# A bidirectional mLSTM and neighbourhood-attention layer on one core: masks by POOL's selection, convolutions that pause at two places, token-major tiles evicted in pairs

## The chip, the cores and the metric

The kernel runs on one core of one Trainium2 chip. The metric is the device time of one execution in microseconds (us). The kernel before was timed three times: median 2721.96 us, lowest 2721.62, highest 2723.16. Durations below come from one profiled execution of it, whose own time was 2718.74 us, with a span from first to last instruction of 2717.0 us.

Engines are named as in the profile: PE is TensorE's matrix multiplication and PEld its weight load; DVE is VectorE, ACT is ScalarE, POOL is GpSimd, SP is SyncE, which issues most DMAs.

## What is computed

One encoder layer runs over two sequences, a prompt of 1024 tokens (s=0 in the code) and a sample of 2048 (s=1), each with 16 learned meta tokens in front. One input projection feeds two branches; their gated outputs are projected, merged and projected again. Cut to its core:

```python
xn = _rmsnorm(h, g_pre)
proj = xn @ w_in + b_in
na_q, na_k, na_v, na_z, ml_qk, ml_v, ml_z, ml_o, ml_g, mg = split(proj)
ya = (neighbourhood_attention(na_q, na_k, na_v, na_rpb) * silu(na_z)) @ w_a
yb = (mlstm_branch(ml_qk, ml_v, ml_g, ml_o, conv_w, head_g) * silu(ml_z)) @ w_b
ga, gb = split(sigmoid(mg), 2)
out = h + _rmsnorm((ga * ya + gb * yb) @ w_out, g_post)
```

In the mLSTM branch, q and k first go through a convolution of three taps and a silu. Then, for each of 4 heads and each of two directions, in chunks along the sequence:

```python
logD = where(lower, b[:, None] - b[None, :] + ig[None, :], NEG)
S = (q @ k.T) * exp(logD - m_t[:, None])
num = S @ v + e_inter * (C @ q)
den = sum(S) + e_inter * (n @ q)
h = num / maximum(abs(den), exp(-m_t))
```

The two directions are added, gated by a sigmoid, and normalised per head (mean and variance over 128 features). `where(lower, ...)` is what the text calls the mask. In the kernel it is applied to the exponent: entries outside the triangle become about -1e30, so that their exponential is 0.

## The kernel before

**Numbers.** Values are float32, and a product of two of them is made as three matmuls of parts: each operand is split into a high part (a copy in the type `fp32r`, made by ACT) and a low part (the difference, made by DVE). In the trace a split shows as a pair such as `whi`/`wlo`, `xh`/`xl`, `sh`/`sl`, `vh`/`vl`.

**Two streams on PE.** A dense stream (`PLAN`) does the projections: first the group of s=0 with a few column blocks, then a stream of seven-product units (`sstream`, L1036 on, where a 2 by 2 block product is made of seven products instead of eight) for the other columns of s=0, then groups of s=1 in two halves of 1024 tokens, and at the end the output projections. A sparse stream (`STEPS`) does the mLSTM of s=0, the attention of s=0, the mLSTM of s=1 and the attention of s=1. `run` takes pieces of both in turn, by costs written in the code, and what comes out is PE's order.

**What sets the order.** PE's instructions stay in the order in which the code is run. The order on the other engines is made by a list scheduler, which simulates the program with durations of its own; an instruction given to `self.behind` stays in program order among its engine's. So an edit that leaves PE alone can still rearrange DVE, ACT, POOL and SP.

**Beside the dense stream.** After each piece of dense work the code calls `beside` (L530). It advances up to two convolutions of q and k (`cprep`, L1546, by `pstep`, L1588): a load, a scaled copy on ACT (L1567), two multiply-adds on DVE (L1570), a tanh on ACT (L1572), a product on DVE (L1574), and stores. It makes one step per call, and a second once a result of the first group of s=1 exists.

**Token-major tiles** (`tm_unit`, L619). For columns that are stored with tokens on partitions, a tile of 128 tokens by 256 or 264 columns is summed in a PSUM bank of 512 words (tag `pj`, three banks). For s=1 DVE adds the bias and moves the tile to SBUF (`stT<-pj,bb`, L661), one tile at a time, two into each `stT` buffer. Of the columns of the attention's values, POOL then issues eight DMAs per buffer (`nv<-stT`, L1034).

**Splitting x at a group change** (`build_half`, L512 to 518): four steps, each with a copy on ACT and a subtraction on DVE (`xh`, `xl`).

**mLSTM outputs** (`ml_outputs`, L1721). A head's sequence is cut into blocks of 256 tokens (two chunks of 128). For each block and both directions at once, 128 partitions by 2 chunks by 2 directions by 128:

- `load`: q and k, the values, and by DMA a broadcast of the decay exponents into `um`.
- `mask` (L1758): DVE adds `trim`, the two triangles of 0 and -1e30, to `um`, pinned by `self.behind`. `trim` is loaded once per sequence from the input `trimask`.
- `decay` (L1764): four exponentials on ACT, in place in `um`.
- `scores` (PE, L1799 and L1801), read out as `ss` (L1803, L1804).
- `weigh`: the product `um<-um,ss` (DVE, L1813), split into `sh` (ACT, L1814) and `sl` (DVE, L1815).
- `back` (PE): `tr` from the state, `sm` from `sh`, `sl` and the values; then `num` (ACT L1829, DVE L1834).
- `finish`: the denominators (L1841 to L1844) and `hb` (L1851, L1852). After every second block `ml_norm` (L1895 on) normalises 512 tokens: `hb<-tog,hb`, four BATCH_NORM_STATS2 and four BATCH_NORM_AGGREGATE, a reciprocal root by twelve tiny operations, `nb` (L1912), four `hb` on ACT (L1914), and a last product with `szg` on DVE (L1915).

The blocks overlap: while block b-1 is in `back`, block b is in `scores` and `weigh`, and block b+1 in `mask` and `decay`.

Of the kernel before, what the change touches and what calls it, by code (L numbers as in the profile page):

```python
# [10 lines left out]
F32 = mybir.dt.float32  # L11
# [3 lines left out]
ALU = mybir.AluOpType  # L15
# [3 lines left out]
P = 128  # L19
TCARGS = dict(schedule_with_timeline_sim=True)  # L20
D = 1024
KT = D // P
# [6 lines left out]
BIG = 1e30  # L29
# [97 lines left out]
class K:  # L127
# [3 lines left out]
    def __init__(self, tc, ins, outs):  # L131
        self.tc, self.nc = tc, tc.nc
        self.xs = []
        self.i, self.o = ins, outs
        self.wreq, self.wraw, self.wrdy, self.wout = deque(), deque(), deque(), 0
        self.wseen, self.wkept, self.xkept = set(), {}, {}
        self.rwait = {}
        self.xput, self.turn, self.last, self.turns = deque(), 0, None, False
        self.need, self.gpost = False, None
        self.pq, self.pact = deque(), deque()  # L140
        self.have, self.rtag = {}, "tr"
        self.fmend = {C_MK + 3 * P: "a", C_NK + 3 * P: "k", C_NQ + 3 * P: "q", C_NZ + 3 * P: "z"}
        self.bg, self.XF, self.XS, self.sb, self.staged = deque(), {}, {}, {}, deque()
        self.hold, self.early = deque(), True
        self.rpre, self.xhold = {}, True


    def rsqrt8(self, pool, v, shape):
# [292 lines left out]
    def build_half(self, s, t0, res):  # L441
# [26 lines left out]
        if s == 0:  # L468
            xts = self.xnext or [self.xtload(s, t0, e, wp, 4) for e in range(4)]
            self.xnext = None  # L470
            while self.rwait:
                yield "wait"
            self.early = False
            yield "scaled"
            g = self.gpre
            if not self.done:
                p = self.psum("sm", [P, 512])
                nc.tensor.matmul(p[:, :KT], self.ident, g, start=True, stop=True)
                g = self.cp.tile([P, KT], F32, name="gx")
                nc.vector.tensor_copy(g, p[:, :KT])  # L480
            x, r = self.xparts(), []
            for e in range(4):
                self.xsplit(x, xts[e], e, 0, g)
                if not self.done:
                    self.wflush(2)
                yield
            res.append(tuple(x))
            if self.done:
                return
            yield from self.rsum(self.toks, r)  # L490
            nc.vector.tensor_copy(self.rc[:, 4:8], r[0])
            dg = self.rdiag(r[0], self.toks[0][0])

            def rows():
                self.rrows(dg, self.rr[:, 1], "sm")
                self.xp.close()
            self.rwait[s, t0] = rows
        else:
            xts = [self.xtload(s, t0, e, wp, 4) for e in range(4)]
            yield  # L500
            yield
            rr = wp.tile([P, 512], F32, name="rx", tag="thT", bufs=1)
            self.rrows(self.rpre.pop((s, t0)), rr, self.rtag)
            yield
            for k in range(KT):
                v = xts[k // 2][:, k % 2]
                self.behind(nc.vector.scalar_tensor_tensor(v, v, self.gpre[:, k:k + 1], rr, op0=ALU.mult, op1=ALU.mult))
                if k % 2:
                    yield
            yield "scaled"  # L510
            x = self.xparts(t0 % 1024 == 0)
            for e in range(4):  # L512
                h = x[0][:, 2 * e:2 * e + 2, :512]
                self.behind(nc.scalar.activation(h, xts[e], AF.Copy))
                self.behind(nc.vector.tensor_tensor(x[1][:, 2 * e:2 * e + 2, :512], xts[e], h.bitcast(F32), op=ALU.subtract))
                yield
            res.append(tuple(x))
            self.xkeep(s, t0, x)

# [10 lines left out]
    def beside(self):  # L530

        self.turn += 1
        self.pstep()
        if (1, 0) in self.have:
            self.pstep()
        if self.bg and self.turn % 2 == 0:
            if next(self.bg[0], "end") == "end":
                self.bg.popleft()
        if self.xput and self.turn % 2 and not self.xhold:
            self.behind(self.nc.sync.dma_start(*self.xput.popleft()))  # L540
# [78 lines left out]
    def tm_unit(self, col, halves, wd):  # L619
# [9 lines left out]
                todo.append((x, s, 0, NM, 1, None))  # L629
        for j, (x, s, c, n, cnt, tok) in enumerate(todo):  # L630
            st = wp.tile([P, 2, WU], F32, name="stT", bufs=4)
            for a in range(cnt):
                p = self.psum("pj", [P, 512])
                o = p[:n, :wd]
                xs = slice(c + a * P, c + a * P + n)
                for k in range(KT):
                    wh, wl = ws[k // 4][0][:, k % 4, :], ws[k // 4][1][:, k % 4, :]
                    if tok is None:
                        both = [(p[:48, :wd], self.xmm[:, k, :], wh), (o, self.xmm[:, k, :NM], wl)]
                        for y, (out, lhs, rhs) in enumerate(both if k < KT - 1 else both[::-1]):  # L640
                            nc.tensor.matmul(out, lhs, rhs, start=k == y == 0, stop=k == KT - 1 and y == 1, skip_group_check=True)
                    else:
                        xh, xl = x[0][:, k, xs], x[1][:, k, xs]
                        nc.tensor.matmul(o, xh, wh, start=k == 0, stop=False)  # L644
                        nc.tensor.matmul(o, xh, wl, start=False, stop=False)  # L645
                        nc.tensor.matmul(o, xl, wh, start=False, stop=k == KT - 1)  # L646
                    if k == 3:
                        if j == len(todo) - 1 and a == cnt - 1:
                            self.wdone()
# [7 lines left out]
                elif s == 0:  # L657
                    r = tok // P + a
                    nc.vector.scalar_tensor_tensor(st[:n, a, :wd], p[:n, :wd], self.rc[:n, r:r + 1], bb[:n, :wd], op0=ALU.mult, op1=ALU.add)
                else:  # L660
                    nc.vector.tensor_tensor(st[:n, a, :wd], p[:n, :wd], bb[:n, :wd], op=ALU.add)  # L661
                if a == cnt - 1:
                    self.tm_store(col, wd, s, n, cnt, tok, st)
                yield 12 * C256
# [371 lines left out]
    def sstream(self, visits, nxt):  # L1036
# [9 lines left out]
        for n, u in self.sorder(visits):  # L1046
# [15 lines left out]
                            self.sstage(*visits[v + 1][:2], w)  # L1062
            q = self.sq[n]
            if u == 7 and not n:
                self.sbload(1)
            tm = c in TMAJ
            form = ("p (k c) -> p k c", dict(k=4)) if tm else ("p (a k c) -> p a k c", dict(a=2, k=4))
# [95 lines left out]
    def group(self, s, t0, meta, cols, reuse, nxt):  # L1163
# [4 lines left out]
        for j, (kind, c) in enumerate(jobs):  # L1168
# [21 lines left out]
            for hf in range(2):  # L1190
# [2 lines left out]
                    side = self.spread(self.build_half(*todo[1][:2], self.xs), 15)  # L1193
                elif last and nxt and nxt[0] == "S":
                    if hf == 0:
                        while self.bg:
                            if next(self.bg[0], "end") == "end":
                                self.bg.popleft()
# [398 lines left out]
    def ml(self, s):  # L1597
# [3 lines left out]
        with tc.tile_pool(name=f"mg{s}", bufs=1, side="right", reuse_waits="tile") as keep:  # L1601
            with tc.tile_pool(name=f"mt{s}", bufs=1, side="right", reuse_waits="tile") as mp:
                self.tri = keep.tile([P, 2, P], F32, name="tri")
                nc.sync.dma_start(self.tri, self.i["tri"])
                self.trim = keep.tile([P, CB, 2, P], F32, name="trim")
                for j in range(CB):
                    nc.sync.dma_start(self.trim[:, j], self.i["trimask"])
                g = []
                yield from self.ml_gates(s, keep, mp, g)
            with tc.tile_pool(name=f"ml{s}", bufs=1, side="right", reuse_waits="tile") as mp:  # L1610
# [110 lines left out]
    def ml_outputs(self, mp, s, h, g, NB, sts, norms):  # L1721
# [33 lines left out]

        def mask(b):
            if b < NB:
                self.behind(nc.vector.tensor_tensor(ums[b], ums[b], self.trim, op=ALU.add))  # L1758

        def decay(b):  # L1760
            if b < NB:
# [505 lines left out]
```

## Time and profile before

| | |
|---|---|
| median of 3 runs | 2721.96 us (2721.62 to 2723.16) |
| profiled execution | 2718.74 us |
| its span | 2717.0 us, 47583 instructions |
| mean granted clock of PE | 0.998 of full speed |
| DMA | 657.53 MB, mean 242 GB/s |

The page's next lines give the chain of work that ended last, followed back from the last instruction, in shares of the span:

```profile
PE 88%; DMA 7%; DVE 2%; ACT 2%; issue 1%; SPq 1%; POOL 0%; DVEq 0%; ACTq 0%; POOLq 0%
```

A row of a timeline begins with the start and the duration in us; then come engine, source line, operation and tiles (out<-in). Brackets give the time for which the engine had been idle ahead of it, and what ended that. Rows of groups give the count, the busy time with the mean ns of one, and the idle time with its releasers.

### The profile page before, as it was taken

How to read it: one execution, taken by the hardware profiler on the slowest of the kernel's cores; microseconds unless marked ns; L12 is line 12 of the kernel's file. 1: busy time of each engine (PE TensorE's matmuls, PEld its weight loads, DVE VectorE, ACT ScalarE, POOL GpSimd, SP SyncE). 2: the span in 40 equal slices, each digit the busy share in tenths (PEclk: the TensorE clock that was granted, in tenths of full speed). 3: DMA queues.
4: the chain of work that ended last, by engine and by line, in shares of the span. 5: the costliest groups of instructions: out<-in, count | busy, mean ns of one | idle time of the engine just before them, and what ended most of it. 6: DMA issues, size and time to landing. Idle time of an engine off the chain costs nothing.

```text
span 2717.0 us, 47583 instructions
## 1 busy us (share of the span) xinstructions
PE 2686.7 (99%) x16696; PEld 2394.5 (88%) x16696; DVE 1766.1 (65%) x4376; ACT 1520.2 (56%) x3375; POOL 126.0 (5%) x294
## 2 busy tenths in 40 slices
PE   9999999999999999999999999999999999999998
PEld 7999988879998889998878888888879898989988
DVE  5557765535777747775424857574658879687864
ACT  5233354435555656666535757564648686767641
POOL 0005000005000013000000000000000000000000
PEclk9999999999999999999999999999999999999999
DMA  9984454369865797757486666786599999898955
GB/s 369 340 283 143 138 187 158 102 239 343 265 222 174 264 325 227 229 175 234 144 294 191 222 202 209 262 278 201 163 299 332 313 298 295 245 317 244 324 208 220
DMA packets 351507, 657.53 MB, mean 242 GB/s; under 512 B 53444, under 2 KB 158868, under 8 KB 351268
## 3 DMA queue, kind: packets, MB, share of 16 engines
q1 hardware_dynamic: 344004, 645.46, 71.7%
q0 software_dynamic: 7264, 9.04, 1.2%
q8 instruction: 131, 2.15, 0.3%
q14 instruction: 108, 0.88, 0.1%
HBM read 438.64 MB, written 215.66 MB: 241 GB/s over the span
## 4 chain that ended last, share of the span: by engine, by line
PE 88%; DMA 7%; DVE 2%; ACT 2%; issue 1%; SPq 1%; POOL 0%; DVEq 0%; ACTq 0%; POOLq 0%
PE pj L172 14%; PE pj L173 14%; PE pj L174 14%; PE pj L644 5%; PE pj L645 5%; PE pj L646 5%; PE sm L1407 3%; PE pj L2042 2%; PE pj L2044 2%; PE pj L2043 2%; PE tr L1393 2%; PE sm L174 2%; PE sm L173 2%; PE sm L172 2%; DMA wraw<-wu 1%; DMA wlo<-wl 1%
## 5 line engine op out<-in xcount | busy, mean ns | idle before, releaser
L172 PE MATMUL pj<-xh,whi 128*128 128x512 f32 (+1 forms) x1480 | 580.2, 392 | 4.6 <-ACT st L569 3.6
L173 PE MATMUL pj<-xl,whi 128*128 128x512 f32 (+1 forms) x1480 | 565.8, 382 | 0.2 <-DVE xl L345 0.2
L174 PE MATMUL pj<-xh,wlo 128*128 128x512 f32 (+1 forms) x1480 | 565.1, 382 | 0.3 <-DVE wlo L272 0.3
L644 PE MATMUL pj<-whi,xh 128*128 128x256 f32 (+1 forms) x1152 | 330.9, 287 | 0.0
L174 PEld LDWEIGHTS pj<-xh,wlo 128*128 128x128 f32 x1480 | 278.2, 188 | 58.2 <-DVE wlo L272 0.6
L172 PEld LDWEIGHTS pj<-xh,whi 128*128 128x128 f32 x1480 | 278.5, 188 | 54.1 <-ACT st L569 4.4
L645 PE MATMUL pj<-wlo,xh 128*128 128x256 f32 (+1 forms) x1152 | 325.0, 282 | 0.6 <-DMA wlo<-wl 0.6
L646 PE MATMUL pj<-whi,xl 128*128 128x256 f32 (+1 forms) x1152 | 324.8, 282 | 0.0
L173 PEld LDWEIGHTS pj<-xl,whi 128*128 128x128 f32 x1480 | 278.8, 188 | 46.2 <-issue 0.7
L2042 PE MATMUL pj<-whi,mh 128*128 128x256 f32 x768 | 220.3, 287 | 0.0
L645 PEld LDWEIGHTS pj<-wlo,xh 128*128 128x128 f32 x1152 | 217.1, 188 | 0.9 <-DMA wlo<-wl 0.8
L644 PEld LDWEIGHTS pj<-whi,xh 128*128 128x128 f32 x1152 | 217.3, 189 | 0.4
L646 PEld LDWEIGHTS pj<-whi,xl 128*128 128x128 f32 x1152 | 217.0, 188 | 0.0
L2043 PE MATMUL pj<-wlo,mh 128*128 128x256 f32 x768 | 217.0, 283 | 0.0
L2044 PE MATMUL pj<-whi,mlo 128*128 128x256 f32 x768 | 216.9, 282 | 0.0
L1396 DVE TENSOR_TENSOR pts<-tr,pts 96x384 fp32r<-96x384 f32 (+2 forms) x192 | 118.5, 617 | 64.7 <-ACT pts L1395 63.8
L172 PE MATMUL pj<-yh,whi 128*128 128x512 f32 x384 | 154.2, 401 | 1.8 <-DVE tg L2009 1.1
L173 PE MATMUL pj<-yl,whi 128*128 128x512 f32 x384 | 151.0, 393 | 0.2 <-DVE yl L1420 0.2
L174 PE MATMUL pj<-yh,wlo 128*128 128x512 f32 x384 | 151.0, 393 | 0.0
L2043 PEld LDWEIGHTS pj<-wlo,mh 128*128 128x128 f32 x768 | 146.1, 190 | 1.0
L2042 PEld LDWEIGHTS pj<-whi,mh 128*128 128x128 f32 x768 | 146.0, 190 | 1.0
L2044 PEld LDWEIGHTS pj<-whi,mlo 128*128 128x128 f32 x768 | 145.9, 190 | 0.0
(459 smaller groups left out, 6171.7 us busy)
## 6 DMA issues: line engine op xcount, KB each, us to landing
whi<-wh SPq DMA_DIRECT2D x140, 512.0 KB
wlo<-wl SPq DMA_DIRECT2D x140, 512.0 KB
wraw<-wu SPq DMA_DIRECT2D x64, 512.0 KB
wh<-whi SPq DMA_DIRECT2D x64, 512.0 KB
wl<-wlo SPq DMA_DIRECT2D x64, 512.0 KB
gt<-st SPq DMA_DIRECT2D x96, 256.0 KB
tg<-gt SPq DMA_DIRECT2D x96, 256.0 KB
xt<-xt SPq DMA_DIRECT2D x32, 512.0 KB
```

Source lines behind the costliest of these rows:

```text
L172: mm(out, ah, bh, start=start, stop=False, **more)
L173: mm(out, ah, bl, start=False, stop=False, **more)
L174: mm(out, al, bh, start=False, stop=stop, **more)
L644: nc.tensor.matmul(o, xh, wh, start=k == 0, stop=False)
L645: nc.tensor.matmul(o, xh, wl, start=False, stop=False)
L646: nc.tensor.matmul(o, xl, wh, start=False, stop=k == KT - 1)
L1393: nc.tensor.transpose(pt[:ks, ch, :], pr_[:, ch * ks:(ch + 1) * ks], self.ident)
L1396: nc.vector.tensor_tensor(pts[:ks, :nb, 1, :], pt[:ks, :nb], pts[:ks, :nb, 0, :].bitcast(F32), op=ALU.subtract)
L1407: nc.tensor.matmul(av[:, cb % 2], vt[:ks, kc // 8 + ch].rearrange("p a b -> p (a b)"), pts[:ks, ch].rearrange("p a b -> p (a b)"), start=c ...
L2042: nc.tensor.matmul(o, mh[:, f, xs], q, start=fresh and f == 0, stop=False, skip_group_check=True)
L2043: nc.tensor.matmul(o, mh[:, f, xs], w[1][:, k, :], start=False, stop=False, skip_group_check=True)
L2044: nc.tensor.matmul(o, ml[:, f, xs], q, start=False, stop=f == KT - 1, skip_group_check=True)
```

## The change

Three edits, and what the scheduler makes of them:

1. **Masks.** The addition of `trim` on DVE, 48 times 128x512, is replaced by `affine_select` on POOL, one for each direction of a block: 96 of 128x2x128. Each compares an affine function of partition and column with 0 and writes -1e30 where it is negative. They aren't pinned. The `trim` tile and its four loads go. POOL gets one more instruction ahead of the first select, which loads a library (the row `ISA`).
2. **Pauses.** A flag `quiet` stops the convolution steps of `beside` at two places: from the first half of the last unit of the group ahead of the seven-product stream until that stream's unit 7 of its first column block, and in the four steps that split x at a group change of s=1. In return, there is a third step per call once the mLSTM of s=0 is done.
3. **Pairs.** For s=1 and columns up to 256 wide, two token tiles share one PSUM bank, and DVE evicts both with one instruction of 128x2x256: 48 in place of 96 of 128x256.

PE keeps its instructions and their order. Three places of the other engines' lists:

**First place: POOL, the start of the first mLSTM** (names: `nv` is the store of the attention's values, `st` a state tile, `um` the exponents). Before:

```order
L1613 MEMSET va_6112 128x2
L1614 MEMSET va_6112 128x2
L1706 MEMSET st 128x130
L1034 DMA nv_244<-stT 8x8x128 x40
L1706 MEMSET st 128x130
L1034 DMA nv_244<-stT 8x8x128 x24
```

And now:

```order
L1711 MEMSET st 128x130
L1040 DMA nv_244<-stT 8x8x128 x24
L1765 ISA
L1765 AFFINE_SELECT um<-um 128x2x128 x2
L1040 DMA nv_244<-stT 8x8x128 x8
L1765 AFFINE_SELECT um<-um 128x2x128 x2
L1040 DMA nv_244<-stT 8x8x128 x32
L1765 AFFINE_SELECT um<-um 128x2x128 x4
```

The selects of the first blocks stand among the 64 DMA issues: 24 ahead of the first mask, 32 ahead of the second, all 64 ahead of the third and fourth.

**Second place: DVE, the start of the seven-product stream** (`cp` is a convolution, `sn` the first product's eviction, `wlo` the low part of a combined weight, `xl` that of a combined x). Before:

```order
L261 TENSOR_TENSOR wlo<-b_1815,whi 128x1024
L837 TENSOR_TENSOR b_1815<-b_1817,b_1815 128x1024
L557 TENSOR_TENSOR pj<-pj,rr 128x512
L1570 SCALAR_TENSOR_TENSOR cp<-cp,cw 128x272
L837 TENSOR_TENSOR t_2242<-b_1839,b_1815 128x1024
L1570 SCALAR_TENSOR_TENSOR cp<-cp,cw 128x272 x2
L959 TENSOR_TENSOR sn<-pj,bb 128x512
L1570 SCALAR_TENSOR_TENSOR cp<-cp,cw 128x272
L261 TENSOR_TENSOR wlo<-t_2242,whi 128x1024
```

And now:

```order
L843 TENSOR_TENSOR b_1815<-b_1817,b_1815 128x1024
L558 TENSOR_TENSOR pj<-pj,rr 128x512
L843 TENSOR_TENSOR t_2212<-b_1839,b_1815 128x1024
L261 TENSOR_TENSOR wlo<-t_2212,whi 128x1024
L558 TENSOR_TENSOR pj<-pj,rr 128x512
L261 TENSOR_TENSOR wlo<-b_1815,whi 128x1024
L558 TENSOR_TENSOR pj<-pj,rr 128x512
L261 TENSOR_TENSOR wlo<-b_2216,whi 128x1024
L778 TENSOR_TENSOR xl<-xt,xh 128x2x512
L965 TENSOR_TENSOR sn<-pj,bb 128x512
```

The four convolution operations are gone from there, and `wlo<-t` follows its `t` at once, ahead of `sn`.

**Third place: DVE and ACT, blocks 1 to 3 of the first head of the first mLSTM.** DVE before, from the eviction of a dense tile on (`ss` and `sc` are scores, `hb` the output of blocks 0 and 1; the row `um<-um,ss` is the product of block 2):

```order
L1844 RECIPROCAL den<-den 128x4
L1804 TENSOR_TENSOR ss<-ss,sc 128x256
L661 TENSOR_TENSOR stT<-pj,bb 128x264
L1852 SCALAR_TENSOR_TENSOR hb<-num,den,hb 128x128
L1813 TENSOR_TENSOR um<-um,ss 128x512
L1852 SCALAR_TENSOR_TENSOR hb<-num,den,hb 128x128
L1815 TENSOR_TENSOR sl<-um,sh 128x512
```

Now, from the next dense tile's eviction on, ahead of the product of block 2:

```order
L664 TENSOR_TENSOR stT<-pj,bb 128x264
L1859 SCALAR_TENSOR_TENSOR hb<-num,den,hb 128x128
L1906 SCALAR_TENSOR_TENSOR hb<-tog,hb 128x512
L1910 BN_STATS bs<-hb 128x6 x4
L1912 BN_AGGR mv<-bs 128x2 x4
L1914 TENSOR_SCALAR mv<-mv 128x4
```

then the tiny operations of the reciprocal root, of which the last and what follows are:

```order
L158 SCALAR_TENSOR_TENSOR nwy<-nwt,nwy 128x4
L1919 SCALAR_TENSOR_TENSOR nb<-mv,nwy 128x4
L1922 TENSOR_TENSOR hb<-hb,szg 128x512
L1820 TENSOR_TENSOR um<-um,ss 128x512
L1822 TENSOR_TENSOR sl<-um,sh 128x512
```

The whole normalisation, 23 instructions from `hb<-tog,hb` to `hb<-hb,szg`, has come ahead of the product of block 2. On ACT the exponentials of block 3 and `sh` of block 2 stood thus before:

```order
L1764 ACTIVATE um<-um,g_a_5902 128x128 x2
L1764 ACTIVATE um<-um,g_a_5908 128x128 x2
L1803 ACTIVATE ss<-sc 128x256
L1851 ACTIVATE hb<-num,den 128x128 x2
L432 ACTIVATE xsq,ss<-xr 128x1024
L689 ACTIVATE stT<-stT 128x528
L1814 ACTIVATE sh<-um 128x512
```

And now the exponentials of blocks 2 and 3, with `sh` of block 2:

```order
L1836 ACTIVATE num<-tr,g_eT_6066 128x130
L1921 ACTIVATE hb<-hb,nb,nwy 128x128 x4
L1771 ACTIVATE um<-um,g_a_5899 128x128 x2
L1771 ACTIVATE um<-um,g_a_5905 128x128 x2
L1771 ACTIVATE um<-um,g_a_5899 128x128 x2
L1771 ACTIVATE um<-um,g_a_5905 128x128 x2
L1821 ACTIVATE sh<-um 128x512
```

They stand behind the four `hb` of the normalisation. The order of all engines from the last third of the second mLSTM to the end is as before.

The diff:

```diff
@@ K.__init__
-        self.rpre, self.xhold = {}, True
+        self.rpre, self.xhold, self.quiet = {}, True, False
@@ build_half (s=1)
             x = self.xparts(t0 % 1024 == 0)
+            self.quiet = True
             for e in range(4):
...
                 yield
+            self.quiet = False
@@ beside
-        self.pstep()
-        if (1, 0) in self.have:
+        for _ in range(0 if self.quiet else 1 + ((1, 0) in self.have) + (("ml", 0) in self.done)):
             self.pstep()
@@ tm_unit
+            pair = s and tok is not None and 2 * wd <= 512
             for a in range(cnt):
-                p = self.psum("pj", [P, 512])
-                o = p[:n, :wd]
+                if not pair or not a:
+                    p = self.psum("pj", [P, 512])
+                o = p[:n, wd * a:wd * a + wd] if pair else p[:n, :wd]
...
-                        nc.tensor.matmul(o, xh, wh, start=k == 0, stop=False)
+                        nc.tensor.matmul(o, xh, wh, start=k == 0 and not (pair and a), stop=False, skip_group_check=True)
...
-                else:
+                elif not pair:
                     nc.vector.tensor_tensor(st[:n, a, :wd], p[:n, :wd], bb[:n, :wd], op=ALU.add)
+                elif a:
+                    two = bb[:, :wd].rearrange("p (t c) -> p t c", t=1).to_broadcast([P, 2, wd])
+                    nc.vector.tensor_tensor(st[:, :, :wd], p[:, :2 * wd].rearrange("p (t c) -> p t c", t=2), two, op=ALU.add)
@@ sstream
             if u == 7 and not n:
+                self.quiet = False
                 self.sbload(1)
@@ group (last unit ahead of "S")
                     if hf == 0:
+                        self.quiet = True
@@ ml
-                self.trim = keep.tile([P, CB, 2, P], F32, name="trim")
-                for j in range(CB):
-                    nc.sync.dma_start(self.trim[:, j], self.i["trimask"])
@@ ml_outputs
         def mask(b):
             if b < NB:
-                self.behind(nc.vector.tensor_tensor(ums[b], ums[b], self.trim, op=ALU.add))
+                for d in range(2):
+                    u = ums[b][:, :, d]
+                    nc.gpsimd.affine_select(u, u, [[0, CB], [1 - 2 * d, P]], ALU.is_ge, -BIG, base=0, channel_multiplier=2 * d - 1)
```

More of the change, by code (lines that the diff above doesn't have):

```diff
@@ L643, in tm_unit @@
                         xh, xl = x[0][:, k, xs], x[1][:, k, xs]
[L644 to L646 removed]
+                        nc.tensor.matmul(o, xh, wh, start=k == 0 and not (pair and a), stop=False, skip_group_check=True)
+                        nc.tensor.matmul(o, xh, wl, start=False, stop=False, skip_group_check=True)
+                        nc.tensor.matmul(o, xl, wh, start=False, stop=k == KT - 1, skip_group_check=True)
                     if k == 3:
```

## The prediction

> **What bounds the kernel now.** The page's busy shares come first, then the busy time by stage, cut where the kernel's own stages change: dense start to 212 us, seven-product stream to 565, first mLSTM (s=0) to 950, first attention to 1365, second mLSTM to 1975, second attention and output projection to the end. Columns: stretch, its length, then busy us of PE, PEld, DVE, ACT and POOL, the granted clock and the DMA share.
>
> ```profile
> PE 2686.7 (99%) x16696; PEld 2394.5 (88%) x16696; DVE 1766.1 (65%) x4376; ACT 1520.2 (56%) x3375; POOL 126.0 (5%) x294
> ...
> 0.00:212.00 212.00, 203.78 (x1348) 184.40 (x1349) 114.38 (x214) 85.93 (x143) 6.39 (x28) 1.00 0.90 325
> 212.00:565.00 353.00, 353.00 (x2016) 307.21 (x2015) 232.35 (x328) 158.13 (x234) 36.92 (x84) 1.00 0.48 155
> 565.00:950.00 385.00, 383.92 (x2664) 353.21 (x2663) 249.96 (x770) 205.34 (x515) 39.40 (x80) 1.00 0.73 248
> 950.00:1365.00 415.00, 414.44 (x2800) 382.23 (x2799) 248.28 (x584) 248.94 (x509) 37.53 (x74) 1.00 0.68 220
> 1365.00:1975.00 610.00, 608.06 (x3138) 509.44 (x3137) 366.98 (x1185) 352.59 (x920) 2.32 (x18) 1.00 0.69 226
> 1975.00:2717.00 742.00, 723.53 (x4741) 658.02 (x4739) 554.15 (x1299) 469.26 (x1055) 3.42 (x10) 0.99 0.87 283
> ```
>
> TensorE is the bound, at full clock. Its whole idle time is 2717.0 - 2686.7 = 30.3 us: 8.2 in the first stretch, 18.5 in the last, 1.1 and 1.9 in the two mLSTM stretches, 0.6 in the first attention, none in the stream. The change leaves TensorE's instructions and their order as they were. So it can win only a part of 30.3 us, and it loses wherever something that TensorE waits for comes later. Work taken from VectorE (65% busy) is no gain in itself.
>
> **Convolutions that pause (start of the seven-product stream).** The one place where the removed work stands ahead of TensorE:
>
> ```profile
> 207.99 0.50 DVE L1570 SCALAR_TENSOR_TENSOR cp<-cp,cw 128x272 f32<-128x272 f32 x1 [0.17 <-ACT cp L1567]
> 208.41 0.68 DVE L959 TENSOR_TENSOR sn<-pj,bb 128x512 f32<-128x512 f32 x1
> 209.01 0.49 DVE L1570 SCALAR_TENSOR_TENSOR cp<-cp,cw 128x272 f32<-128x272 f32 x1
> 209.24 0.36 PE L1079 MATMUL pj<-whi,xh 128*128 128x256 f32 x1 [0.89 <-DVE sn L959]
> 209.42 1.22 DVE L261 TENSOR_TENSOR wlo<-t,whi 128x1024 fp32r<-128x1024 f32 x1
> 210.69 0.38 PE L1080 MATMUL pj<-wlo,xh 128*128 128x256 f32 x1 [1.09 <-DVE wlo L261]
> ```
>
> TensorE sits 0.89 us for a weight part and a freed bank, and 1.09 us for `wlo`. Ahead of both, ACT and VectorE do convolution steps (0.50 and 0.49 us on VectorE, 0.17 waited for ACT). With the pause the splits `wlo` stand ahead of `sn` (second place of the change). I take both waits as gone: **-2.0** us. Bounds: 0 if the weight load itself is late, -2.0 at most, since there is nothing more to win here. The later catch-up (a third step once the first mLSTM is done) falls where TensorE idles 1.9 us in 610, on engines 58 to 60% busy (352.59 and 366.98 of 610.00): 0. The pause while x is split at the group change, four units of work long, I put at 0, bounds -0.6 and +1, by the 0.6 us idle in the stretch 950 to 1365.
>
> **Masks on POOL.** What leaves VectorE, and who waited for it:
>
> ```profile
> L1758 DVE TENSOR_TENSOR um<-um,trim 128x512 f32<-128x512 f32 x48 | 32.8, 683 | 5.1 <-DMA um<-ud 5.1
> ACT um L1764 <- DVE um L1758: 22.0, 22, 3.6
> 647.93 0.69 DVE L1758 TENSOR_TENSOR um<-um,trim 128x512 f32<-128x512 f32 x1 [1.51 <-DMA um<-ud]
> 656.61 0.68 DVE L1813 TENSOR_TENSOR um<-um,ss 128x512 f32<-128x512 f32 x1
> ```
>
> 48 adds of 0.683 us, 32.8 us of VectorE, go; 96 selects of 128x256 come. No row shows a select, so its price is bounded by POOL's nearest rows:
>
> ```profile
> L1706 POOL MEMSET st<- 128x130 f32 x8 | 1.7, 208 | 532.5 <-DVE ccl L1792 521.8 <-PE sm L173 10.7
> L1178 POOL CAST xmm<-xh 128x128 fp32r<-128x128 f32 x2 | 0.6, 350 | 3.2 <-ACT xh L391 3.2
> 171.00 1.28 POOL L587 COPY km<-st 128x16 f32<-128x16 f32 x1
> 171.01 1.22 DVE L772 TENSOR_TENSOR r0l<-xt,r0h 128x1024 fp32r<-128x1024 f32 x1
> ```
>
> The memset writes 130 elements a partition in 0.208 us and reads nothing: low end 0.2. The cast reads and writes 128 in 0.350; twice that is 0.7, the value I take, as the row with the most alike work. The copy of 16 elements took 1.28 us, exactly while VectorE ran a 1.22 us operation with two SBUF inputs: POOL can be held up for about that long. High end 0.35 + 1.28 = 1.6. Two selects a block then take 1.4 us (0.4 to 3.2) where the add took 0.68, so a mask comes some 0.7 us later. Cover: between the first mask at 647.93 and the product that needs its exponentials (656.61) lie 8.7 us; mask 0.7, exponentials 1.3 (ACT row below) leave 6.7. A library load for POOL, new ahead of the first select, has no row either; it stands behind 24 of the DMA issues and before `um` has landed at 647.9, in idle time. I put all of this at **+1.0** for TensorE, a small share of the 48 blocks being tight (bounds: 0, and the slow case among the rivals).
>
> The Trainium skill speaks against this move: its page "GPSIMD Engine Reference", section 1 (Specifications), says that POOL's SBUF interfaces are shared with VectorE and contended when a VectorE instruction has two SBUF inputs. The 1.28 us copy agrees. The same page, section 2.1 (Instruction dispatch), gives about 6 us for the first call of a freshly loaded kernel; no run here shows that, and by it, as an estimate, the sum stays the same, because the load lies in idle time of POOL.
>
> **Pairs.** 96 evictions of 128x256 at 0.42 us become 48 of 128x512 at the 0.68 of the `sn` row:
>
> ```profile
> L661 DVE TENSOR_TENSOR stT<-pj,bb 128x256 f32<-128x256 f32 x96 | 40.3, 420 | 27.9 <-PE pj L646 26.2 <-DMA nv<-stT 0.6
> ```
>
> 40.3 - 32.6 = 7.7 us of VectorE saved. VectorE waited for TensorE ahead of these (26.2 us), not the other way, so TensorE gains **0**; one bank held for two tiles costs nothing as long as the eviction follows within the next tile. Bounds -1.1 (all idle of that stretch) and +1.
>
> **What the new order costs.** With less work on VectorE the scheduler sets the first head of the first mLSTM out differently (third place of the change, VectorE and ACT): the product `um<-um,ss` of block 2 now stands behind the whole normalisation of query block 0, and ACT's exponentials of blocks 2 and 3 behind the four normalising `hb`. TensorE uses `sh` of block 2 in the first matmul of this list:
>
> ```profile
> 683.59 0.23 PE L172 MATMUL sm<-vh,sh 128*128 128x130 f32 x1
> ...
> 681.50 0.43 DVE L661 TENSOR_TENSOR stT<-pj,bb 128x264 f32<-128x264 f32 x1
> 681.92 0.35 DVE L1852 SCALAR_TENSOR_TENSOR hb<-num,den,hb 128x128 f32<-128x128 f32 x1
> 682.66 0.68 DVE L1899 SCALAR_TENSOR_TENSOR hb<-tog,hb 128x512 f32<-128x512 f32 x1
> 684.26 0.86 DVE L1903 BATCH_NORM_STATS2 bs<-hb 128x6 f32<-128x128 f32 x4
> 685.37 0.30 DVE L1905 BATCH_NORM_AGGREGATE mv<-bs 128x2 f32<-128x6 f32 x3
> 686.17 0.17 DVE L1905 BATCH_NORM_AGGREGATE mv<-bs 128x2 f32<-128x6 f32 x1
> 686.97 0.17 DVE L154 TENSOR_SCALAR nwy<-nwy 128x4 int32<-128x4 int32 x1
> 687.17 0.16 DVE L156 SCALAR_TENSOR_TENSOR nwt<-nwy 128x4 f32<-128x4 f32 x1
> 685.59 0.65 DVE L1815 TENSOR_TENSOR sl<-um,sh 128x512 fp32r<-128x512 f32 x1
> ...
> 692.59 1.64 ACT L1914 ACTIVATE hb<-hb,nb,nwy 128x128 f32<-128x128 f32 x4
> 671.39 1.28 ACT L1764 ACTIVATE um<-um,g_a 128x128 f32<-128x128 f32 x4 [1.33 <-DVE um L1758]
> 675.00 0.62 ACT L1814 ACTIVATE sh<-um 128x512 fp32r<-128x512 f32 x1
> ```
>
> In the run before, `sh` of block 2 was made at 675.00, 8 us early. In the new order the eviction of the dense tile at 681.50 stands ahead of the chain, and it can't come sooner, as TensorE fills that tile just then. From it on VectorE: eviction 0.43, `hb` 0.35, `hb<-tog,hb` 0.68, statistics 0.86, aggregates 0.30 + 0.17, then 13 tiny dependent operations 0.20 apart (686.97 to 687.17), 2.6: 5.4 us. On ACT: four `hb` 1.64, exponentials of blocks 2 and 3 at 1.28 each (the product of block 2 runs beside the second), `sh` 0.62: 4.8. A row begins some 0.08 us before the recorded end of the one ahead (`sn` above ends at 209.09, the next row begins at 209.01); eight such hand-overs take off 0.6. `sh` is there at 681.5 + 5.4 + 4.8 - 0.6 = 691.1. TensorE arrives at 683.59: a wait of 7.5. And `sl` (0.65, from `sh`) holds the third matmul of the group another 0.5, the first two filling the rest: **+8.0**, bounds 7 and 9.5 by the hand-overs. It doesn't hang on POOL: the last stores of NV are evicted and issued long before,
>
> ```profile
> 667.68 2.23 POOL L1034 DMA_DIRECT2D nv<-stT  x4 [0.23 <-DVE stT L661]
> ```
>
> so that with the eight issues of this eviction (at 0.56 each to 672.2) four selects even at 1.28 end at 677.3, when the exponentials can't start before 688.
>
> A long wait also costs clock behind it, as the one long wait of the last stretch shows:
>
> ```profile
> 2335.70:2339.30 3.60, 0.26 (x3) 0.02 (x1) 1.99 (x6) 3.54 (x9) 0.00 (x0) 1.00 1.01 195
> 2339.30:2342.70 3.40, 3.15 (x14) 3.16 (x15) 2.87 (x7) 3.40 (x12) 0.00 (x0) 0.50 1.04 222
> 2332.72 1.06 ACT L1344 ACTIVATE kd<-kr 64x1024 fp32r<-64x1024 f32 x1 [3.47 <-DMA kr<-nkm]
> ```
>
> After 3.3 us of idle TensorE ran 3.4 us at clock 0.50: 1.7 us lost. The new wait is longer, so **+1.7** once.
>
> **Sum.** -2.0 + 1.0 + 0 + 8.0 + 1.7 = +8.7 us on the profiled execution: 2718.74 + 8.7 = 2727.4. That execution lies 3.2 us below the median of the three runs; on the median, 2721.96 + 8.7 = **2730.7**, 0.32% slower. A measurement of this kernel can tell about 0.2% (5.4 us) from no change: slower is above 2727.4, faster below 2716.5.
>
> **The rivals.**
> *The tail gives it back (not slower).* The 3.3 us wait at 2335.7 and its 1.7 of half clock come from a `kr` load that landed late under a DMA share above 1. If the loads of the tail, shifted by the wait, fall apart again, 5.0 to 5.3 us go: 8.7 - 5.3 = +3.4, 2725.4. Against it: loads and TensorE shift together, and the order in the tail is the same on all engines. It decides if that load lands 3.3 us sooner against TensorE. 0.17.
> *The wait is half as long (not slower):* if ACT's and VectorE's chain starts earlier than I read, 4.0 and no half clock behind it, - 2.0 + 1.0 = +3.0, 2725.0. The eviction ahead of it stands against this. 0.04.
> *POOL is slow.* Selects held up by VectorE at 1.6 each put a mask 2.5 us later (3.2 for 0.68). The 6.7 us of cover hide that at the first block, but ACT waited for a mask 22 times, up to 3.6 us, so in these blocks it stood right behind. If a quarter of them, six, pass 2 us on to TensorE, it is +12 over the sum, 2742.7; if all 22 do, +44. The rule cited above is this rival's mechanism. It decides at a select above about 1.2 us, where a mask is 1.7 late. 0.12.
> *Faster (the change does what a relieved VectorE suggests, and the new order's wait doesn't appear, and the tail's goes):* -2.0 - 5.3 = -7.3, 2714.7. Only 30.3 us of idle exist at all, and both must happen. 0.05.
>
> **How the numbers follow.** Forecast 0.62, between 2728 and 2734 by the terms' own bounds. Slower: 0.62 + 0.12 = 0.74; within 0.2%: 0.17 + 0.04 = 0.21; faster 0.05. The range holds the forecast, both milder rivals (with 3 us for the start that doesn't gain or gains and for the spread of runs, 1.5) and the middle of the slow one: 2722 to 2743.
>
> **What would show it.** In the profile after: no wait of TensorE at `pj<-whi,xh` and `pj<-wlo,xh` near 209; one wait of 7 to 9 us near 683 (less the 2 us won before) at `sm<-vh,sh`, released by ACT's `sh`, with a stretch at half clock behind; selects at 0.4 to 1.0 us; idle of the later mLSTM stretch still near 2 us; the tail's wait for `kr` still there. I am wrong if `sh` of block 2 is ready before 684, if selects take over 1.2 us, or if TensorE waits for masks.

## The result and the profile after

| | before | with the change |
|---|---|---|
| median (runs) | 2721.62 us (5) | 2740.42 us (5) |
| lowest to highest | 2716.11 to 2723.16 | 2734.56 to 2746.08 |
| profiled execution, its span | 2718.74, 2717.0 us | 2740.42, 2738.5 us |

The ratio is 1.0076, 95% interval 1.0055 to 1.0097: slower by 18.8 us, where 9 were forecast. (Two single runs of nearly twice the time, 4979.61 us in e10 and 5337.15 us in the kernel before beside e5 to e8, are outside all ratios.) The page's busy shares of the changed kernel, then the three stretches that changed (columns as in the prediction):

```profile
PE 2695.3 (98%) x16696; PEld 2401.0 (88%) x16696; DVE 1743.9 (64%) x4280; ACT 1516.5 (55%) x3375; POOL 167.4 (6%) x390
```

and its windows:

```profile
565.00:950.00 385.00, 375.17 (x2608) 346.21 (x2607) 231.56 (x694) 198.29 (x501) 54.86 (x111) 0.99 0.70 239
950.00:1365.00 415.00, 409.47 (x2758) 378.27 (x2758) 253.45 (x585) 248.10 (x514) 37.41 (x74) 0.99 0.70 223
1365.00:1975.00 610.00, 605.46 (x3106) 505.52 (x3105) 341.05 (x1108) 342.35 (x896) 28.75 (x80) 1.00 0.67 221
```

TensorE's idle time went from 30.3 to 2738.5 - 2695.3 = 43.2 us, and its busy time, for the same matmuls, from 2686.7 to 2695.3. So the 21.5 us of span are 12.9 of waits and 8.6 in which the same matmuls kept TensorE busy longer. Of these 8.6, half clock behind the two longest waits makes 6.3, as shown below; the rest is in small pieces, such as matmuls that follow each other more slowly behind a short wait. Idle are 9.8 of 385 in the first mLSTM (1.1 before), 5.5 of 415 in the first attention (0.6) and 4.5 of 610 in the second mLSTM (1.9).

To see where it was lost, the same matmul is looked up in both timelines. TensorE's order is the same, so the difference of the starts is the delay up to there. Before:

```profile
785.59 0.39 PE L174 MATMUL sm<-vwh,kt 128*128 128x260 f32 x1 [0.34 <-DVE kt L1691]
1395.45 0.44 PE L1483 MATMUL sm<-g_lf,ones 128*1 128x68 f32 x4 [0.25 <-ACT g_aR L1476]
1717.82 0.39 PE L172 MATMUL sm<-vwh,kt 128*128 128x260 f32 x1 [0.33 <-ACT kt L1690]
2628.37 0.49 PE L172 MATMUL pj<-yh,whi 128*128 128x512 f32 x1 [0.67 <-ACT yh L1419]
```

With the change:

```profile
794.05 0.39 PE L174 MATMUL sm<-vwh,kt 128*128 128x260 f32 x1 [0.60 <-DVE kt L1696]
1412.85 0.44 PE L1491 MATMUL sm<-g_lf,ones 128*1 128x68 f32 x4 [0.25 <-ACT g_aR L1484]
1739.52 0.39 PE L172 MATMUL sm<-vwh,kt 128*128 128x260 f32 x1 [0.33 <-ACT kt L1695]
2650.18 0.49 PE L172 MATMUL pj<-yh,whi 128*128 128x512 f32 x1 [0.67 <-ACT yh L1427]
```

The delay is 8.5 us in the first mLSTM's second half, 17.4 at the start of the second mLSTM, 21.7 in its middle, 21.8 near the end. There are three losses, then, and the tail adds nothing. (The first is net of 2.9 us won ahead of it.)

**First loss, 8.5 us: the forecast one.** TensorE, ACT and POOL of the changed kernel around it:

```profile
688.38 0.48 PE L172 MATMUL sm<-vh,sh 128*128 128x130 f32 x1 [7.53 <-ACT sh L1821]
...
683.83 1.65 ACT L1921 ACTIVATE hb<-hb,nb,nwy 128x128 f32<-128x128 f32 x4 [2.31 <-DVE nb L1919]
685.38 2.43 ACT L1771 ACTIVATE um<-um,g_a 128x128 f32<-128x128 f32 x8
687.72 0.61 ACT L1821 ACTIVATE sh<-um 128x512 fp32r<-128x512 f32 x1
...
670.68 1.47 POOL L1765 TENSOR_SCALAR_AFFINE_SELECT um<-um 128x256 f32<-128x256 f32 x4
```

And its windows right behind the wait:

```profile
688.00:692.00 4.00, 3.58 (x15) 3.40 (x16) 3.13 (x11) 2.27 (x5) 0.00 (x0) 0.50 0.68 239
692.00:696.00 4.00, 4.00 (x23) 4.00 (x23) 2.04 (x10) 0.74 (x3) 0.00 (x0) 0.58 0.19 66
```

POOL had masked blocks 2 and 3 by 672.2. Their eight exponentials ran 13 us later, behind the four `hb` of the normalisation, and `sh` came 7.5 us late. Behind the wait the granted clock was 0.50 for 4 us and 0.58 on the mean of the next 4: 3.58 us of matmuls at 0.50 and 4 us at 0.58 lose about 3.5 us, not 1.7.

**Second loss, 8.9 us: the first attention.** No wait at all was forecast here. The chain of the changed kernel up to its second wait (start, duration, what):

```profile
1039.78 9.90 DMA cpl<-mq
1049.69 0.02 issue
1049.71 0.62 ACT cpl L1575
1050.34 0.03 issue
1050.36 0.63 DVE cpl L1578
...
1053.83 0.43 DVE yg L1422
```

Both waits in TensorE's timeline:

```profile
1026.87 0.74 PE L1415 MATMUL sm<-pts,vt 96*128 96x256 f32 x4 [1.18 <-ACT prb L1384]
1054.39 1.19 PE L1415 MATMUL sm<-pts,vt 96*128 96x256 f32 x4 [4.35 <-DVE yg L1422]
```

And the windows behind the second wait:

```profile
1054.40:1058.00 3.60, 3.60 (x17) 3.60 (x18) 2.71 (x6) 3.07 (x8) 1.28 (x3) 0.50 0.49 151
1058.00:1060.00 2.00, 2.00 (x10) 2.00 (x10) 1.16 (x3) 1.29 (x2) 2.00 (x4) 0.50 0.70 190
1060.00:1062.00 2.00, 2.00 (x17) 2.00 (x16) 1.69 (x5) 1.71 (x5) 1.15 (x3) 0.86 0.80 228
```

A convolution's load was in flight for 9.9 us. The convolution's first operation stood on ACT ahead of what the attention needed; VectorE took its multiply-adds and then the `yg` for which TensorE waited. With three steps a call the steps come closer together, and the distance between load and first use, counted in steps, is shorter in time: between 950 and 1365 us the median from a load's issue to the copy on ACT that reads it is 7.0 us with the change (7.0 in e1 too) and 15.8 before (16.5 in e2), when loads and copies are paired in order. Half clock again: 5.6 us at 0.50, 2.8 lost, and a little more in the third window.

**Third loss, 4.3 us: the second mLSTM.** SP's issue (SPq), POOL, ACT and TensorE of the changed kernel:

```profile
1607.99 0.73 SPq L1741 DMA_DIRECT2D um<-ud  x1
1615.04 0.77 POOL L1765 TENSOR_SCALAR_AFFINE_SELECT um<-um 128x256 f32<-128x256 f32 x2 [77.03 <-DMA wraw<-wu]
1615.48 1.28 ACT L1771 ACTIVATE um<-um,g_a 128x128 f32<-128x128 f32 x4 [3.64 <-POOL um L1765]
1616.66 0.36 ACT L1695 ACTIVATE kt<-tr 128x256 fp32r<-128x256 f32 x1
...
1617.07 0.39 PE L172 MATMUL sm<-vwh,kt 128*128 128x260 f32 x1 [1.74 <-ACT kt L1695]
```

The exponents land at about 1614.8, and ACT waits for them with `kt` behind it, on which TensorE depends: 1.74 us here, and 0.54 in the same way at 1473.63. In the kernel before, the addition was pinned on VectorE, and the exponentials of a new head stood behind the last `kt` on ACT. The selects aren't pinned, so the scheduler put the exponentials of two blocks further forward, ahead of the last two `kt`. Over the whole kernel ACT waited 77.7 us for POOL's masks, 39 times and up to 7.6, where it had waited 22.0 us for VectorE's.

### The profile page after: what moved, and what is told of

Read it like the earlier page. It is cut to its first block, busy times and chain, and to the rows that moved or that the text cites. A ratio compares the mean times of both kernels' runs of the same rounds, so it can differ in the third digit from the quotient of the medians.

```text
span 2738.5 us, 47731 instructions
## 1 busy us (share of the span) xinstructions
PE 2695.3 (98%) x16696; PEld 2401.0 (88%) x16696; DVE 1743.9 (64%) x4280; ACT 1516.5 (55%) x3375; POOL 167.4 (6%) x390
## 4 chain that ended last, share of the span: by engine, by line
PE 85%; DMA 9%; DVE 3%; ACT 2%; issue 1%; SPq 0%; DVEq 0%; POOL 0%; POOLq 0%; ACTq 0%
PE pj L172 14%; PE pj L173 14%; PE pj L174 14%; PE pj L647 5%; PE pj L648 5%; PE pj L649 5%; PE pj L2049 2%; PE pj L2051 2%; PE pj L2050 2%; PE sm L1415 2%; PE sm L174 2%; PE sm L173 2%; PE tr L1401 2%; PE sm L172 2%; DMA vr<-nv 1%; PE tr L174 1%
```

## The experiments

Each run gives its ratio to the kernel before on the same chip, with the 95% interval. 0.10% is 2.7 us. The kernel before had medians of 2718.50 to 2719.57 us there, 2 to 3 under the 2721.62 above, so ratios are compared, not times. The record's edits are shown cut to what matters (`...`); where masks return to VectorE, the `trim` tile and its loads return too.

**e1: masks back on VectorE.**

```diff
-                for d in range(2):
-                    nc.gpsimd.affine_select(ums[b][:, :, d], ...)
+                self.behind(nc.vector.tensor_tensor(ums[b], ums[b], self.trim, op=ALU.add))
```

> The change with its first edit undone: masks are added on VectorE again, pauses, third step and pairs stay. Theory (two separate causes: the masks on POOL make the 7.5 us wait at 688 in the first mLSTM, the third convolution step makes the 4.35 us wait at 1054 in the first attention): the wait at 688 is gone, with its half clock, so about 9.7 us less than the change; the wait at 1054 stays. About 2730 against 2721.6 before and 2740 for the change. Rival (all of it comes from the masks, the wait at 1054 only follows from the shift of the first one): both waits are gone, 2719 to 2721.

2718.84 us, 1.0002 (0.9991 to 1.0012). The masks on POOL are nearly all of the loss: 0.74%. The wait at 688 is gone. The expectation, 2730, was some 8 us over the kernel before and so 8 too high, since the attention's waits fell too, though not to nothing. The longer one in TensorE's timeline,

```profile
1015.31 1.22 PE L1415 MATMUL sm<-pts,vt 96*128 96x256 f32 x4 [2.51 <-ACT prb L1384]
```

and the head of the chain:

```profile
1003.01 7.09 DMA cpl<-mk
1010.10 0.02 issue
1010.12 0.04 ACTq L1575
1010.16 0.05 issue
1010.21 0.63 ACT cpl L1575
```

It is the same mechanism, a convolution's load for which ACT waits, at another place and shorter. Neither theory had it so: the cause is there without the masks, and how much it costs depends on where the load falls.

**e2: no third step.**

```diff
-        for _ in range(0 if self.quiet else 1 + ((1, 0) in self.have) + (("ml", 0) in self.done)):
+        for _ in range(0 if self.quiet else 1 + ((1, 0) in self.have)):
```

> The change without the third convolution step per call (one step, two once the first result of s=1 exists, as before); masks on POOL, pauses and pairs stay. Theory of two causes: the wait at 688 stays at 7.5, the waits at 1027 and 1054 (1.2 and 4.35 with their half clock) are gone: 9 us less than the change, about 2731. Rival (all from the masks): the wait at 1054 stays, within 2 us of the change, about 2740.

2731.98 us, 1.0056 (1.0038 to 1.0074). Both waits of the first attention are gone, 7.5 at 688 stays, as the theory of two causes had it. The gain by the ratios, 0.20% or 5.4 us, is short of the 9 expected; the intervals of e2 and of the change overlap, so it is rough.

**e3: both edits of e1 and e2,** that is pauses and pairs alone.

> The change with masks on VectorE and without the third step: pauses and pairs alone. Both theories: no wait at 688. Theory of two causes: no wait at 1054 either, and the two waits at 209 gone: 2 us under before, about 2719.5. If a wait of over 2 us in the first attention is left, the third step isn't its cause.

2715.25 us, 0.9987 (0.9976 to 0.9998): no wait over 0.4 us in the first attention, none at 209. Against e1 the third step costs 0.15%, against e2 the masks cost 0.69%.

**e4: masks on POOL alone,** with convolutions and tiles as before.

```diff
+        for _ in range(1 + ((1, 0) in self.have)):
...
+            pair = False
```

> The kernel before with the masks moved to POOL alone (convolutions as before, single tiles). Theory: the order of VectorE and ACT in the first mLSTM suffers here too, though differently: two waits for sh of about 2 and 3.9 us in 668 to 688 by the place of the instructions in the new order, the waits at 209 stay, no wait at 1054: 6 to 9 us slower than before, 2728 to 2731. Rival (the selects cost nothing by themselves; the wait at 688 needs the pairs or the pauses): as before, 2721.6.

2739.61 us, 1.0072 (1.0057 to 1.0087). The rival, that pairs or pauses are needed for the loss, falls; but 6 to 9 us over the kernel before were expected, and 0.72% is near 20. The two waits for `sh` in the first mLSTM came in 2.4 and 3.7 us, as the order had it; what was left out are the half clock behind each, the waits for `kt` in the second mLSTM (1.5 here), and a wait of 2.5 us in the first attention. That one ends a chain with a convolution's load of 7.3 us, at the old step rate: a shift alone can bring such a load late, and the third step makes it likelier, not first possible. Not all of the 0.72% need be the masks': by 565 us, ahead of any select, this profile is already 5.2 us behind the one before, with waits of 0.77 and 0.88 at 202 to 204, of 1.24 and 1.10 at 212 to 213, and 6.8 us at half clock behind them.

**e5: exponentials pinned** (with the edit of e2).

```diff
-                        nc.scalar.activation(ums[b][:, j, d], ums[b][:, j, d], AF.Exp, ...)
+                        self.behind(nc.scalar.activation(ums[b][:, j, d], ums[b][:, j, d], AF.Exp, ...))
```

> The change without the third step (2732.0 in the run before), and with the exponentials on ACT pinned behind the instruction that the code issued before them, so that in the second mLSTM they no longer stand ahead of kt. Theory (the masks cost twice by order: in the first mLSTM the wait of 7.5 us at 688, in the second the waits for kt at 1603 and 1611, 0.4 + 2.25 us, because exponentials that wait for a late load of um stand ahead of kt on ACT): the kt waits of the second mLSTM fall to what the kernel before has (0.3), the wait at 688 stays: 2.3 us of waits and up to 1.7 of half clock less, about 2728 to 2730. Rival (the kt waits come from late loads whatever the order): same as without the pin, 2732.

2724.67 us, 1.0022 (1.0013 to 1.0032), clear of e2. TensorE's waits for `kt` on ACT, from the waits of both, e2 first and then e5:

```profile
PE sm L172 <- ACT kt L1695: 4.2, 5, 2.3
```

```profile
PE sm L172 <- ACT kt L1695: 0.5, 2, 0.3
```

So the order on ACT made the third loss. The gain of 0.34%, 9 us, is more than the 3.7 us of these waits. In the two profiled runs the second mLSTM got 6.7 us shorter, of which idle time is 3.8. A further 2.6 us lie between the wait at 688 and its start, where e2's wait of 0.85 for `kt` at 885 is gone as well: 9.3 together. (Behind that the two profiles don't compare: e2's is its slowest run, 2742.19 us, with a wait of 4.58 at 2226.)

**e6: stores of nv on SP** (with the edit of e2). **e7: e6 with e5's pin.**

```diff
-                    self.nc.gpsimd.dma_start(dst, st[r * 64:r * 64 + 64, a, q * P:q * P + P])
+                    self.nc.sync.dma_start(dst, st[r * 64:r * 64 + 64, a, q * P:q * P + P])
```

> The change without the third step, and with the stores of nv issued by SP in place of POOL, so that nothing stands ahead of the selects on POOL. Theory (the wait at 688 is made by the order of VectorE and ACT, in which the scheduler puts the product of block 2 behind the normalisation because it takes the masks to be late behind 64 DMA issues; with these gone it puts them early): no wait at 688, 7.5 + 0.3 us of idle and 3.5 of half clock less, 11 under 2732, so about 2721, unless the 128 issues of half a us on SP delay loads. Rival (POOL's selects are late by themselves, or the library load is): the wait at 688 stays.

> The change without the third step, with both mends: stores of nv on SP and pinned exponentials. Theory: neither the wait at 688 nor the kt waits of the second mLSTM: about 2717 to 2719, like pauses and pairs with masks on VectorE (2715.3), so the selects on POOL cost nothing once the order is right. Rival (the selects cost by themselves): over 2725.

2769.87 us, 1.0192 (1.0176 to 1.0208), and 2764.07, 1.0170 (1.0153 to 1.0187): both totals missed by far. The wait of 7.5 for `sh` is gone in both, 1.5 us is the most that is left. In its place the dense stream waits (e6, timeline of TensorE and SP):

```profile
697.96 0.59 PE L647 MATMUL pj<-whi,xh 128*128 128x264 f32 x1 [14.02 <-DVE stT L664]
...
681.58 7.86 SPq L1040 DMA_DIRECT2D nv<-stT  x8
```

and from the chain that ends at that wait:

```profile
691.44 6.01 DMA bb<-b_in
```

Eight issues took SP 7.9 us, about 1 us each, against 0.56 on POOL; the bias `bb` of the next unit was issued behind them and landed at 697.45; the tile's eviction waited for it, and TensorE for the tile's bank. A second wait, at 1107, is 20 us. So these runs show that with nothing ahead of the selects on POOL the scheduler orders the first mLSTM well, but they can't say what selects cost, since they add a new bound.

**e8: pairs alone.**

> The kernel before with pairs alone: masks on VectorE, convolutions as before. As predicted: pairs are worth 0, the two waits at 209 (0.9 + 1.1) stay: as before, within 0.5 us. If pairs are worth something by themselves, up to 3.3 us less (what pauses and pairs together gave).

2717.74 us, 1.0001 (0.9990 to 1.0013): worth nothing, as predicted. The waits at 209 are there (1.06 and 1.09), and behind them this profile has a stretch at half clock, which the one before doesn't have:

```profile
211.40:214.90 3.50, 3.50 (x19) 3.50 (x18) 3.50 (x5) 3.48 (x5) 0.00 (x0) 0.51 0.56 180
```

**e9: normalisation behind the product** (on top of e5).

```diff
-            nc.vector.tensor_tensor(um, um, both, op=ALU.mult)
+            self.lastw = nc.vector.tensor_tensor(um, um, both, op=ALU.mult)
...
-        nc.vector.scalar_tensor_tensor(hb, to, 1.0, hb, op0=ALU.add, op1=ALU.mult)
+        x = nc.vector.scalar_tensor_tensor(hb, to, 1.0, hb, op0=ALU.add, op1=ALU.mult)
+        self.tc.add_manual_dep(x.ins, self.lastw.ins.name, NoSync)
```

> The run with pinned exponentials (e5, 2724.7), and one edge of order more: the normalisation's first instruction on VectorE stands behind the latest product um<-um,ss. Masks stay on POOL, and the stores of nv with them. Theory (the wait at 688 is order on VectorE and ACT, not POOL's time): with the 23 instructions of the normalisation behind the product, 5.4 - 0.4 - 0.7 us of VectorE and 1.6 of ACT leave the chain, and what stays is the eviction, hb, the exponentials and sh: the wait falls from 7.5 to 3 to 4 us, and the clock after it is halved for one stretch less: about 2719 to 2721. Rival (the masks of block 2 are late on POOL): the wait stays at 7.5, 2724.7.

2722.11 us, 1.0009 (0.9999 to 1.0019). The wait, TensorE's row:

```profile
683.74 0.48 PE L172 MATMUL sm<-vh,sh 128*128 128x130 f32 x1 [3.57 <-ACT sh L1821]
```

7.53 became 3.57 with POOL's list unchanged in this part. What is left isn't POOL's time either (POOL and ACT of e9):

```profile
670.36 1.48 POOL L1765 TENSOR_SCALAR_AFFINE_SELECT um<-um 128x256 f32<-128x256 f32 x4
680.73 2.44 ACT L1771 ACTIVATE um<-um,g_a 128x128 f32<-128x128 f32 x8
```

The masks were done at 671.84, the exponentials began 8.9 us later, at their place on ACT: the wait was order. The time fell by 0.13%, a little less than expected, and the intervals of e5 and e9 just overlap.

**e10: masks on POOL in the second mLSTM only** (with e2's and e5's edits). **e11: the same, each of these selects twice.**

```diff
+                if not s:
+                    self.behind(nc.vector.tensor_tensor(ums[b], ums[b], self.trim, op=ALU.add))
-                for d in range(2):
+                for d in range(2 if s else 0):
```

> Pauses and pairs, no third step, exponentials pinned; masks on VectorE in the first mLSTM (where POOL has the stores of nv) and on POOL in the second, 64 selects. Theory (selects cost nothing where the order is right): no wait at 688, kt waits as before: the same as with all masks on VectorE (2715.3, e3), 2714 to 2718. Rival (selects cost by themselves, or the late um loads pass through POOL): 2720 or more.

> As e10, but each select of the second mLSTM is made twice (it changes nothing in the data): POOL's price doubled, 64 more selects of 0.41 us, in an order of the other engines that is the same row for row. Theory: the cover hides it, within 2 us of e10. Rival (POOL is on the path, the slow-POOL rival of the prediction): 0.8 us a block more in the blocks in which ACT waits for the mask, some 10 us or more.

2712.91 us, 0.9983 (0.9972 to 0.9994), and 2714.05, 0.9985 (0.9972 to 0.9998). 64 selects, then 128, on POOL (e10, e11):

```profile
L1771 POOL TENSOR_SCALAR_AFFINE_SELECT um<-um 128x256 f32<-128x256 f32 x64 | 30.2, 496 | 550.4 <-DMA va<-mv 235.0 <-DMA um<-ud 212.3 <-DMA wraw<-wu 74.7
```

```profile
L1771 POOL TENSOR_SCALAR_AFFINE_SELECT um<-um 128x256 f32<-128x256 f32 x128 | 60.3, 505 | 523.2 <-DMA va<-mv 239.5 <-DMA um<-ud 192.7 <-DMA gt<-st 69.8
```

30 us more of POOL changed nothing that can be measured. In the right order the selects are free, at double their price too, and the slow-POOL rival is out for the second mLSTM. VectorE, ACT and TensorE have the same order in both runs, instruction by instruction. They gain nothing either: e10 equals e3, where VectorE adds all masks.

**e12: pauses alone,** without the third step.

> The kernel before with the pauses alone: masks on VectorE, single tiles, no third step. As predicted for the pauses: the waits at 209 gone, 2.0 us less than before, 2716.5; with pairs worth 0 (e8) this equals e3 (2715.3).

2713.70 us, 0.9977 (0.9965 to 0.9989): the fastest ratio, 6 us under the kernel before on its chip, and not to be told from e3 (0.9987), e10 and e11. All four beat both kernels, and the pauses do it.

## Why the prediction was right in its sign and short in its size

- **The new wait (+8.0).** Right: 7.53 us at the matmul named, released by `sh`, in the order read from the lists. e9 shows that it is order. From the dense tile's eviction (678.61) to the end of `sh` (688.33) the chain took 9.7 us, where 9.6 were added up.
- **Half clock (+1.7).** Right in mechanism, mis-sized: 3.5 us behind this wait, and 2.8 behind the one at 1054. The one example of before (3.6 us of wait, 3.4 at 0.50) was taken as the price of any longer wait.
- **Pauses (-2.0).** Right in mechanism, and too small: the waits at 209 are gone with the change, but alone the pauses are worth 0.23% (0.11 to 0.35%), 3 to 9.5 us, more than the bound of 2.0. One part that the sum lacks is the half clock behind these waits in e8, some 1.5 us; how often it happens, and where the rest of the gain is, no run shows.
- **Pairs (0).** Right, by e8.
- **The catch-up by a third step (0).** This step failed: 8.9 us in the profiled run, 0.15 to 0.20% by e1 with e3 and the change with e2. It was put down as work, for engines with time to spare; it is also a shorter distance between a convolution's load and the copy on ACT that waits for it, in a stretch where the three loads looked at took 7.1 to 9.9 us. That issuing the loads earlier would mend it wasn't tried. And it was looked for in the second mLSTM, when it ran in the first attention.
- **Masks on POOL (+1.0).** Mis-sized, and for another reason than its bounds. The select took 0.407 us in the median (0.398 to 1.447, row below), under the 0.7 taken. The cost came from the lost pin: with the exponentials ahead of `kt`, a late load of `um` reached TensorE by way of ACT, 4.3 us in the profiled run, 0.34% by e2 with e5. So the sign that idle time of the second mLSTM would stay near 2 us failed (4.5). The change's description named the pin; the prediction read the order at the first mLSTM only.
- **Rivals.** The tail's wait stayed, at 3.2 us, so that rival is out. The slow-POOL rival gave nearly the right time, 2742.7, for a reason that e11 rules out in the second mLSTM and the early masks rule out at the wait in the first: not POOL's price but places in the order of ACT and VectorE. That 2740.42 lies in the range of 2722 to 2743 is therefore luck: the range reached so far for this rival, and the terms' own band, 2728 to 2734, missed. The rule that speaks against the move, contention with VectorE (the Trainium skill, "GPSIMD Engine Reference", section 1), can't be what cost it: selects took 0.41 in the median and at most 1.45 us, and doubling them in the second mLSTM cost nothing. The trace agrees that VectorE can hold a select up: the longest, from 735.13, ran while VectorE did a subtraction of two SBUF inputs, `wlo<-wraw,whi`, for 1.23 us from 735.09.

The selects of the changed kernel (shortest, median and longest, in ns):

```profile
L1765 POOL TENSOR_SCALAR_AFFINE_SELECT um<-um x96: 398/407/1447, 636.4 to 1967.0; 128x256 f32<-128x256 f32 x96
```

By ratios the sum is: pauses and pairs -0.13%, masks on POOL +0.69%, third step on top +0.20%, together the +0.76% measured. Of the masks' 0.69%, 0.34 is ACT's order, mostly in the second mLSTM (e5), 0.13 the normalisation's place (e9), and the rest, 0.2 to 0.3, goes when the first mLSTM's masks return to VectorE (e10); e9 still waits 3.57 us there.

## What to carry to other kernels

On a kernel that is 99% bound by one engine, work moved off another engine is worth what the bound engine waits for it, here nothing; the order that a list scheduler makes of the rest is what changes the time. So read the new order in every stage in which a moved instruction stands, not at the first one only, and ask of each load in front of an in-order engine what is queued behind it. A pin belongs to the work that waits: where the pinned instruction moves to another engine, pin its consumer.

## What the runs showed of the hardware that was not expected

- After 7.5 us of idle the granted clock stayed at 0.50 for some 7 us, after 4.35 us for some 6, and after 3.6 us (before) for 3.4. The length of the wait alone doesn't set it: behind the 3.57 us of e9 the clock was 0.50 from 683.7 to 690.0, some 6 us, and 0.96 in the 2 us that follow. In the change the two long waits, 11.9 us, cost 6.3 more this way.
- Loading POOL's library took no time that the trace shows: the first selects started 0.09 us after the DMA issue ahead of them ended (rows below). The Trainium skill gives about 6 us for the first call of a freshly loaded kernel ("GPSIMD Engine Reference", section 2.1); this trace doesn't show them.

```profile
631.89 4.44 POOL L1040 DMA_DIRECT2D nv<-stT  x8 [1.53 <-DVE vwl L1677]
636.42 0.84 POOL L1765 TENSOR_SCALAR_AFFINE_SELECT um<-um 128x256 f32<-128x256 f32 x2
```

- The same DMA issue (`nv<-stT`) took about 1 us on SP in e6 (8 in 7.86) and 0.56 on POOL.
